# Two transformer blocks in one kernel: where the weight tiles lie behind the moving tiles, and output projections by three matmuls

## The chip, the cores and the metric

The kernel runs on one core of a Trainium2 chip. The metric is the device time of one execution in microseconds (us), the median of the runs shown. TensorE (PE) does the matmuls, and its weight loads are listed apart (PEld). VectorE (DVE) and ScalarE (ACT) do the elementwise work, GpSimd (POOL) little, and SyncE (SP) issues the weight transfers.

## The reference

Two blocks follow each other on x of 256 tokens by 1024, each of two layers, all in float32.

```python
# first block, per layer
proj = rms_norm(x, norm_mix[l]) @ w_in[l]                # 1024 -> 5120
x = x + (gates * (attention_a @ w_proj_a, attention_b @ w_proj_b)) @ w_out[l]
up = rms_norm(x, norm_ffn[l]) @ w_up[l]                  # 1024 -> 2 x 2816
x = x + (silu(conv(a)) * bval) @ w_down[l]               # 2816 -> 1024
# second block, per layer
y = even_mixer(h) or odd_mixer(h)                        # ends in @ w_out, 1024 -> 1024
x = x + rms_norm_2(y, g[1]);  y = memory_cross_attention(h, mem)
x = x + rms_norm_2(y, g[3]);  y = jnp.square(jax.nn.relu(h @ w1)) @ w2    # 1024 -> 4096 -> 1024
x = x + rms_norm_2(y, g[5])
```

Nearly all of the arithmetic is products of a weight matrix with activations of 256 tokens.

## The kernel before, in words

Activations stand transposed: features on the 128 partitions, 256 tokens along a row. To keep float32 accuracy every operand is split into a rounded part (hi) and a rest (lo), both of type float32r, and a product is hi·hi + lo·hi + hi·lo. `mm3` (L239 to L243) issues these three matmuls of 256 columns for one tile of 128 by 128 weights: weights hi on tokens hi, weights lo on tokens hi, weights hi on tokens lo. In most projections the weights are the stationary operand, which TensorE loads (one LDWEIGHTS for each matmul), and the tokens (`xh`, or `ya`, `yb`, `ox`) are the moving one. `proj_n` is the other way round: weights move, 512 columns at a time.

`plan` lists the 434 weight blocks in the order of use. `prep` (L188 to L201) loads one into a `raw` tile (three buffers, SP's queue), and for each half of it lets ACT write the hi part (L199) and DVE the lo part (L200) of a tile `w`, of which there are WB = 8. `take` hands a block to a projection and prepares blocks up to LEAD = 5 ahead; `hold(True)` stops this at the end of the matrix in work.

The output projections (`w_out`, `w_down`, `ev_out`, `od_out`, `w2`) end in `proj_tail` (L367 to L376): eight chunks of 128 output features, or the last four of `ev_out` and `od_out` (`OutFirst` does their first 512 features by `mm3`, in banks `mo`). Seven of them go through `proj_wide` and `mm3_wide` (L245 to L248), which do one tile of weights by two matmuls: weights hi on 512 columns (tokens hi and lo side by side), then weights lo on 256 columns. The bank `mw` then holds two partial sums, which DVE and ACT add up: `on_part` in `residual` (L871 to L883, additions in L875 and L877) or `Output.part` (L1336 to L1351, a copy by ACT in L1343 and an addition in L1344). The last chunk goes through `proj_c`, by `mm3` in half a bank. A matrix of `w_down` has 22 tiles per chunk, `w2` 32, the others 8.

The order on each engine is made by a scheduler that simulates the program's time line, which may take matmuls of a later chunk ahead of those of an earlier one.

Where tiles lie, as built: a pool gives all buffers of a tag slots of one size, that of the largest tile under the tag. The largest `w` tile is that of a block of 260 columns, 2·2·260·4 = 4160 bytes, which is 16·256 + 64, and the slots begin at byte 39552 of a partition. So the eight slots begin at 128, 192, 0, 64, 128, 192, 0, 64 modulo 256. The tiles of moving tokens are 4096 bytes each: the tag `xs` (input of `w_in`, `w_up`, `w1`) begins at 83072, 128 modulo 256, and `hs` (input of the output projections) at 154944, 64 modulo 256. Rows, halves and columns inside a tile are multiples of 256 bytes apart. So for each weight tile there is one distance "weights behind tokens, modulo 256": 0, 64, 128 or 192, each for about a quarter of the matmuls. For the stretches that the rows below show:

| stretch from (us) | weights at | tokens at | behind | the tile just before |
|---|---|---|---|---|
| 949.46 | 43712 | 95360 | 64 | 128 behind |
| 950.88 | 68672 | 91264 | 192 | 64 behind |
| 952.28 | 60352 | 87168 | 64 | 192 behind |
| 953.64 | 52032 | 83072 | 192 | 64 behind |
| 272.55 (two tiles) | 60352, 43712 | 87168, 83072 | 64 | 192 behind |
| 275.28 | 56192 | 95360 | 0 | 64 behind |
| 276.71 | 47872 | 91264 | 128 | 0 behind |
| 278.14 | 52032 | 87168 | 192 | 128 behind |
| 630.43 | 52032 | 87168 | 192 | 0 behind |
| 1255.94 (two tiles) | 60352, 43712 | 87168, 83072 | 64 | 0 behind |
| 1263.06 (two tiles) | 52032, 68672 | 83072, 95360 | 192 | 128 behind |

Each of these tiles serves 12 matmuls of 256 columns.

Of the kernel before, what the change touches and what calls it, by code (L numbers as in the profile page):

```python
# [32 lines left out]
TWO_PI = (6.28125, 0.0019350051879882812, 3.0199159819567e-07)  # L33
LEAD = 5
WB = 8
TCARGS = dict(schedule_with_timeline_sim=True)
SET_EXP = "natural_log_exp_and_others"

# [77 lines left out]
def starts(blocks):  # L116

    out = [0]
    for _, _, nk, _, C in blocks:
# [1 line left out]
    return out  # L121


BUFS = {"x": 5, "xs": 4, "hs": 16, "ft": 7, "sq": 2, "p": 6, "bias": 3, "row": 4, "sm": 16, "mk": 2, "mv": 2,
        "mm": 2, "sc": 2, "pT": 2, "pv": 1, "ms": 1}


# [1 line left out]
def net(ctx, tc, A, out):  # L129
    nc = tc.nc  # L130
    act, dve, pe, pool = nc.scalar, nc.vector, nc.tensor, nc.gpsimd
    cp = ctx.enter_context(tc.tile_pool(name="const", bufs=1))
    wp = ctx.enter_context(tc.tile_pool(name="wts", bufs=1))
    ap = ctx.enter_context(tc.tile_pool(name="acts", bufs=1))
    pp = ctx.enter_context(tc.tile_pool(name="psum", bufs=1, space=PSUM))
    dp = ctx.enter_context(tc.tile_pool(name="dram", bufs=1, space=DRAM))

    def f(x):
        return x.bitcast(F32)

# [43 lines left out]
    start = starts(W)  # L184
    state = {"n": 0, "next": 0, "limit": len(W), "after": None, "sum": None}
    ready = {}

    def prep(i, pieces=1):  # L188
        name, k0, nk, c0, C = W[i]
        raw = wp.tile([P, nk, C], F32, tag="raw", name=f"raw{i}", bufs=3)  # L190
        src = A["wt"][start[i]:start[i] + P * nk * C].rearrange("(p k c) -> p k c", p=P, k=nk)
        for a in range(0, nk, max(1, nk // pieces)):
            nc.sync.dma_start(raw[:, a:a + max(1, nk // pieces)], src[:, a:a + max(1, nk // pieces)])
        h = max(1, nk // 2)
        ready[i] = []
        for a, b in ((0, h), (h, nk)):
            if a < b:
                w = wp.tile([P, 2, b - a, C], F32R, tag="w", name=f"w{i}", bufs=WB)
                act.activation(w[:, 0], raw[:, a:b], AF.Copy)  # L199
                dve.tensor_tensor(w[:, 1], raw[:, a:b], f(w[:, 0]), op=OP.subtract)  # L200
                ready[i] += [w[:, :, k] for k in range(b - a)]  # L201

    def take(name, c0, k0=0):

        i = state["n"]
        assert (W[i][0], W[i][3], W[i][1]) == (name, c0, k0), (W[i], name, c0, k0)
        state["n"] += 1
        ahead()
        return ready.pop(i)
# [25 lines left out]
    def mm(o, a, b, start, stop):  # L235
        i = pe.matmul(o, a, b, start=start, stop=stop, skip_group_check=True).ins  # L236
        if state["after"] is not None:
            no_sync(i, state["after"])

    def mm3(o, l, r, start, stop=True):  # L240

        for n, (a, b) in enumerate(((0, 0), (1, 0), (0, 1))):
            mm(o, l[:, a], r[:, b], start and n == 0, stop and n == 2)  # L243

    def mm3_wide(o, l, r, start, stop):  # L245

        mm(o, l[:, 0], r, start, False)
        mm(o[:, 0:T], l[:, 1], r[:, 0], False, stop)  # L248

    def cut(w, s):  # L250
        return w[:, :, s]
# [63 lines left out]
    def proj_c(name, c0, x, k=KC, tag="mm"):  # L315

        ps = bank(tag, "mm", (T,))
        for k0 in range(0, k, 8):
            w = take(name, c0, k0)
            for kk in range(min(8, k - k0)):  # L320
                mm3(ps, w[kk], x(k0 + kk), start=(k0 + kk == 0), stop=(k0 + kk == k - 1))
        return ps

    def proj_wide(name, c0, x, k, tag):

        ps = bank(tag, "mw")
        for k0 in range(0, k, 8):
            w = take(name, c0, k0)
            for kk in range(min(8, k - k0)):
                mm3_wide(ps.rearrange("p a t -> p (a t)"), w[kk], x(k0 + kk), start=(k0 + kk == 0),  # L330
                         stop=(k0 + kk == k - 1))
        return ps

    def proj_n(name, c0, x, C=256, tag="mm"):

        if C <= 256:
# [27 lines left out]
        def later(self, k0):  # L364
            return lambda: self(k0)

    def proj_tail(name, x, k, on_part, tags=("mm", "sc", "mm", "sc", "mm", "sc", "mm", "sc"), first=0):  # L367

        for c in range(first, 8):
            if c == 4:  # L370
                hold(True)
            if c < 7:
                ps = proj_wide(name, 128 * c, x, k, tags[c])
                on_part(c, ps[:, 0], ps[:, 1])
            else:
                on_part(c, proj_c(name, 128 * c, x, k, tags[c]), None)  # L376


    xt = A["xT"].rearrange("(k p) t -> p k t", p=P)
    x = [sb("x", f"x{j}") for j in range(4)]  # L380
# [15 lines left out]
    def const(name, shape, q=nc.sync):  # L396
        t = cp.tile(list(shape), F32, name=name)
        q.dma_start(t, A[name])
        return t
# [14 lines left out]
    class Sums:  # L414
# [8 lines left out]
        def part(self, s, last=False):  # L423
            first = self.ps is None
            if first:
                self.ps = bank("ms", "ssum", (T,))
            state["sum"] = pe.matmul(self.ps, ones, s, start=first, stop=last).ins  # L427
# [184 lines left out]
        return t[hh * 64:hh * 64 + 64, c]  # L612


    h = Split("xs")
    for c in range(8):
        split_last = h.chunk(c, x[c // 2][:, c % 2], vcol(V_MIX + c))

    def first_sums():
# [4 lines left out]
        ns.chunk(x[3][:, 1])  # L624
        return ns

    exchange = const("exchange", [P, P], nc.gpsimd)
    table = const("table", [32, 28], nc.gpsimd)
    sink = cp.tile([P, 16], F32, name="sink")
# [38 lines left out]
    for l in range(DEPTH):  # L668
        vb = l * V_L1
        w_in = f"w_in{l}"  # L670
        def rope_unit(nat):
            ra = sb("sm", "ra", (2, 4, 2, 8))
            rb = sb("sm", "rb", (2, 4, 2, 8))
            for i in range(2):
                rt = nat[:, i].rearrange("p (h d) -> p h d", h=4)[:, :, 0:16]
                rt = rt.rearrange("p h (b r) -> p h b r", b=2)
                dve.tensor_tensor(ra[:, i], rt, trig[:, 0, i][:, None].to_broadcast([P, 4, 2, 8]), op=OP.mult)
                for b in range(2):
                    dve.tensor_tensor(rb[:, i, :, b], rt[:, :, 1 - b],
                                      trig[:, 1, i, b][:, None].to_broadcast([P, 4, 8]), op=OP.mult)  # L680
                dve.tensor_tensor(rt, ra[:, i], rb[:, i], op=OP.add)
            pt = bank("pT", "qT")
            for c in range(2):
                for i in range(2):
                    tr(pt[:, c, col(i)], nat[:, i, col(c)])
            s = single("rope", "qTs")
            act.activation(s, pt, AF.Copy)
            return s
# [17 lines left out]
        o = unit(0)  # L706
# [143 lines left out]
        for j in range(4):  # L850
# [3 lines left out]
            for w, y, g, tag in ((pa, ya, gates[j], "mm"), (pb, yb, gates[4 + j], "pT")):  # L854
                o = bank(tag, "mm")
# [9 lines left out]
        def residual(w, y, k, gains):  # L865

            hn = Split("xs") if gains is not None else None
            ns = Sums()
            xn = []

            def on_part(c, a, b):  # L871
                if c % 2 == 0:
                    xn.append(sb("x", f"x{c // 2}"))
                t = xn[c // 2][:, c % 2]
                state["block1"] = dve.tensor_tensor(t, x[c // 2][:, c % 2], a, op=OP.add).ins  # L875
                if b is not None:
                    dve.tensor_tensor(t, t, b, op=OP.add)  # L877
                if c < 6 and c % 2:
                    ns.pair(xn[c // 2])
                if hn is not None:  # L880
                    hn.chunk(c, t, gains(c))
                if c >= 6:
                    ns.chunk(t)  # L883

            proj_tail(w, y, k, on_part)
            hold(False)
            return xn, hn, ns
# [4 lines left out]
        for j in range(11):  # L892
# [6 lines left out]
            a = sb("ft", "fa")  # L899
# [58 lines left out]
    hm = mem_operand(0, mem)  # L958


    lprod = sb("sm", "lp", (64,))
    lsum = sb("sm", "ls", (2,))
    for j in range(2):
        no_sync(dve.tensor_tensor_reduce(lprod, lamv[:, 2 * j], lamv[:, 2 * j + 1], 1.0, 0.0, op0=OP.mult,
# [60 lines left out]
    xn = []  # L1025
# [284 lines left out]
    class Output:  # L1310
# [22 lines left out]
            self.sums.chunk(ps)  # L1333
            self.scale(self.ys[3][:, c % 2], ps, c)

        def part(self, c, a, b):  # L1336
            if b is None:
                self.chunk(c, a)
                return
            if c % 2 == 0:  # L1340
                self.ys.append(sb("ft", "y"))
            y = self.ys[c // 2]
            act.activation(y[:, c % 2], b, AF.Copy)  # L1343
            dve.tensor_tensor(y[:, c % 2], a, y[:, c % 2], op=OP.add)  # L1344
            if c == 6:
                self.sums.chunk(y[:, 0])
                self.scale(y[:, 0], y[:, 0], c)
            elif c % 2:
                self.sums.pair(y)
                for i in range(2):  # L1350
                    self.scale(y[:, i], y[:, i], c - 1 + i)  # L1351

    def close(y, r):

# [14 lines left out]
    for l in range(DEPTH):  # L1369
        name, oo, of = even(h, nrm) if l == 0 else odd(h, nrm)  # L1370
        y = Output(lambda c: gain2(l, 1, c), 2)
        for j in range(2):
            y.pair(j, of.banks[j])
        proj_tail(name, oo, KC, y.part, tags=(None,) * 4 + ("sc", "mm", "sc", "mm"), first=4)
        r = y.sums.rows(1)
        mem_keys(l, hm, mk, 1)
        xn = []
# [156 lines left out]
```

## Time and profile before

| what | us |
|---|---|
| median of 3 runs | 1434.24 (1433.52 to 1435.65) |
| the profiled execution: its time | 1434.43 |
| the profiled execution: its span, from first to last instruction | 1432.3 |
| TensorE busy | 1388.8 |
| DVE busy | 1019.8 |
| ACT busy | 886.3 |

Busy time is the union of an engine's instructions. Matmuls are pipelined: one of 256 columns takes some 283 ns from start to end, and the next starts long before it ends. So what a matmul costs in a stream is read from the starts: of n matmuls in an unbroken row, the row's time less one duration, over n - 1.

### The profile page before, as it was taken

The numbers are of one execution on the slowest core, as the hardware profiler recorded it, in microseconds if no ns is written. First come the engines' busy times: TensorE is split into PE (matmuls) and PEld (weight loads), VectorE is DVE, ScalarE is ACT, GpSimd is POOL, SyncE is SP. The second block draws the span as 40 slices with busy tenths as digits, with TensorE's granted clock in tenths as the row PEclk, the third lists the DMA queues.
The fourth block names the chain that finished last, engine by engine and source line by source line (L and its number), as shares of the span: only waits on it lengthen the run. The fifth ranks groups of instructions, "written<-read, shape, count | busy, mean of one in ns | idle before, by whom it ended". The sixth has DMA issues, their size and how long they took to land.

```text
span 1432.3 us, 26226 instructions
## 1 busy us (share of the span) xinstructions
PE 1388.8 (97%) x9950; PEld 1270.7 (89%) x9950; DVE 1019.8 (71%) x2140; ACT 886.3 (62%) x1740; POOL 27.3 (2%) x54
## 2 busy tenths in 40 slices
PE   8999999999999999999999989899999999899997
PEld 6789999998888999999899968799989878799886
DVE  6665888886656578888777786777656876777554
ACT  6666566665566666666656656566556676576553
POOL 1000000000000000000000010000000010000000
PEclk9999999999999999999999989999999999999999
DMA  7543566556653455656655553266656534265662
GB/s 247 187 124 119 182 195 191 188 177 188 192 170 119 127 172 188 193 190 198 198 167 164 154 139 118 75 190 186 186 187 180 161 94 133 82 186 189 182 189 85
DMA packets 69326, 236.14 MB, mean 165 GB/s; under 512 B 7954, under 2 KB 12322, under 8 KB 69200
## 3 DMA queue, kind: packets, MB, share of 16 engines
q1 hardware_dynamic: 67136, 229.24, 51.6%
q0 software_dynamic: 1920, 5.04, 1.8%
q8 instruction: 78, 1.28, 0.4%
q14 instruction: 48, 0.39, 0.1%
q10 hardware_dynamic: 144, 0.19, 0.0%
HBM read 233.35 MB, written 1.09 MB: 164 GB/s over the span
## 4 chain that ended last, share of the span: by engine, by line
issue 53%; PE 39%; DVE 3%; ACT 3%; DMA 1%; POOL 0%; SPq 0%; DVEq 0%; POOLq 0%; ACTq 0%
PE mm L236 21%; PE mw L236 12%; PE mo L236 2%; PE ssum L427 1%; PE pT L483 1%; PE sc L607 1%; PE sc L604 1%; ACT w L199 1%; DVE w L200 1%; PE pv L541 1%; DMA bias<-brel_d 1%; DMA x<-in_xT_dram 0%; ACT rstd L176 0%; ACT sq L431 0%; ACT px L176 0%
## 5 line engine op out<-in xcount | busy, mean ns | idle before, releaser
L200 DVE TENSOR_TENSOR w<-raw,w 128x512 fp32r<-128x512 f32 (+2 forms) x866 | 585.3, 686 | 303.3 <-ACT w L199 292.8
L199 ACT ACTIVATE w<-raw 128x512 fp32r<-128x512 f32 (+2 forms) x866 | 535.5, 626 | 414.6 <-PE mm L236 225.5
L236 PE MATMUL mm<-xh,w 128*128 128x256 f32 x5892 | 722.8, 283 | 7.8 <-ACT xh L1000 6.8
L236 PEld LDWEIGHTS mm<-xh,w 128*128 128x128 f32 x5892 | 703.7, 190 | 21.2 <-ACT xh L1000 8.4
L236 PE MATMUL mw<-xh,w 128*128 128x512 f32 (+1 forms) x1832 | 327.3, 339 | 2.4 <-DVE xh L271 1.4
L236 PEld LDWEIGHTS mw<-xh,w 128*128 128x128 f32 x1832 | 281.2, 188 | 44.6 <-DVE xh L271 2.0
L236 PE MATMUL mm<-w,xh 128*128 128x512 f32 (+2 forms) x672 | 145.8, 372 | 9.5 <-ACT w L199 7.0
L236 PEld LDWEIGHTS mm<-w,xh 128*128 128x128 f32 x672 | 113.6, 191 | 34.0 <-ACT w L199 8.4
L236 PE MATMUL mo<-xh,w 128*128 128x256 f32 x192 | 30.6, 307 | 0.5 <-ACT xh L513 0.5
L236 PEld LDWEIGHTS mo<-xh,w 128*128 128x128 f32 x192 | 26.5, 206 | 4.4 <-ACT xh L513 1.7
L1000 ACT ACTIVATE xh<-x,vec 128x256 fp32r<-128x256 f32 x48 | 22.6, 501 | 10.4 <-DVE x L1365 9.9
L497 POOL DMA_DIRECT2D bias<-brel_d x28 | 14.9, 538 | 680.0 <-DVE sbb L821 293.0
L905 ACT ACTIVATE ftt<-fa,vec 128x256 f32<-128x256 f32 x44 | 24.1, 594 | 2.3 <-DVE fa L900 0.5
L1003 DVE SCALAR_TENSOR_TENSOR xh<-x,vec,xh 128x256 fp32r<-128x256 f32 x48 | 22.1, 483 | 1.1 <-ACT xh L1000 1.1
L431 ACT ACTIVATE sq<-x 128x512 f32<-128x512 f32 x33 | 20.4, 617 | 2.3 <-DMA x<-in_xT_dram 2.1
L906 DVE SCALAR_TENSOR_TENSOR ftt<-fa,vec,ftt 128x255 f32<-128x255 f32 x44 | 20.9, 482 | 0.2
L907 DVE SCALAR_TENSOR_TENSOR ftt<-fa,vec,ftt 128x254 f32<-128x254 f32 x44 | 21.0, 477 | 0.0
L703 DVE TENSOR_TENSOR gate<-mm,rstd 128x512 f32<-128x512 f32 x16 | 11.1, 691 | 12.5 <-PE mm L236 12.5
L438 DVE TENSOR_TENSOR sq<-sq 128x512 f32<-128x512 f32 x26 | 17.9, 688 | 0.0
L176 ACT ACTIVATE ftt<-ftt 128x512 f32<-128x512 f32 x22 | 13.9, 631 | 6.4 <-DVE ftt L907 6.4
L1364 DVE TENSOR_TENSOR y<-y,rstd 128x512 f32<-128x512 f32 (+1 forms) x25 | 14.5, 581 | 4.3 <-ACT rstd L176 4.1
L910 DVE TENSOR_TENSOR fa<-mm,rstd 128x512 f32<-128x512 f32 x22 | 15.1, 687 | 3.1 <-PE mm L236 3.1
(413 smaller groups left out, 1137.2 us busy)
## 6 DMA issues: line engine op xcount, KB each, us to landing
raw<-in_wt_dram SPq DMA_DIRECT2D x411, 512.0 KB, 3.6
raw<-in_wt_dram SPq DMA_DIRECT2D x16, 384.0 KB, 3.5
bias<-brel_d POOLq DMA_DIRECT2D x28, 128.0 KB, 3.4
raw<-in_wt_dram SPq DMA_DIRECT2D x4, 520.0 KB, 3.5
mem<-in_memT_dram SPq DMA_DIRECT2D x8, 256.0 KB, 4.2
x<-in_xT_dram SPq DMA_DIRECT2D x4, 256.0 KB, 6.7
raw<-in_wt_dram SPq DMA_DIRECT2D x4, 256.0 KB, 3.3
out_dram<-y SPq DMA_DIRECT2D x4, 256.0 KB, 2.5
```

The lines of the kernel that those rows point to most:

```text
L199: act.activation(w[:, 0], raw[:, a:b], AF.Copy)
L200: dve.tensor_tensor(w[:, 1], raw[:, a:b], f(w[:, 0]), op=OP.subtract)
L236: i = pe.matmul(o, a, b, start=start, stop=stop, skip_group_check=True).ins
L431: act.activation(sq, src, AF.Square)
L438: dve.tensor_tensor(self.acc, self.acc, sq, op=OP.add)
L497: nc.gpsimd.dma_start(o, src)
L905: act.activation(t[:, c], a[:, c], AF.Identity, bias=vcol(vb + V_CB + ch), scale=w[2])
L906: dve.scalar_tensor_tensor(t[:, c, 1:], a[:, c, :T - 1], w[1], t[:, c, 1:], op0=OP.mult, op1=OP.add)
L907: dve.scalar_tensor_tensor(t[:, c, 2:], a[:, c, :T - 2], w[0], t[:, c, 2:], op0=OP.mult, op1=OP.add)
L910: dve.tensor_tensor(a, o, over(rr), op=OP.mult)
L1000: act.activation(hi, t, AF.Copy, scale=g)
L1003: return dve.scalar_tensor_tensor(lo, t, g, f(hi), op0=OP.mult, op1=OP.subtract)
```

## The change

Weight slots become 4224 bytes (`W_SLOT` = 1056 elements, 16·256 + 128), so that they begin at 128 and 0 modulo 256 in turn. Two unused tiles (`pad`) of 192 and 64 bytes, and a tag `ro` of its own for three small tiles that made the slots of `sm` large, move the other pools: `xs` then begins at 83776 and `hs` at 150592, both 64 modulo 256. Every weight tile is then 64 or 192 bytes behind the moving tile. `proj_wide` and `mm3_wide` go; `proj_tail` uses `mm3` for every chunk. Chunks 0 to 5 share a bank in pairs, where only the first matmul of the first chunk starts a sum, and 6 and 7 have a bank each. `on_part` gets a pair or a single chunk, and no partial sums are left to add.

```diff
+W_SLOT = 1056
...
-BUFS = {"x": 5, "xs": 4, "hs": 16, "ft": 7, "sq": 2, "p": 6, "bias": 3, "row": 4, "sm": 16, "mk": 2, "mv": 2,
+BUFS = {"x": 5, "xs": 4, "hs": 16, "ft": 7, "sq": 2, "p": 6, "bias": 3, "row": 4, "sm": 16, "ro": 4, "mk": 2, "mv": 2,
...
+    def pad(name, n):
+        ap.tile([P, n // 4], F32, tag=name, name=name, bufs=1)
...
-                w = wp.tile([P, 2, b - a, C], F32R, tag="w", name=f"w{i}", bufs=WB)
+                w = wp.tile([P, W_SLOT], F32R, tag="w", name=f"w{i}", bufs=WB)
+                w = w[:, :2 * (b - a) * C].rearrange("p (s k c) -> p s k c", s=2, k=b - a)
...
-    def mm3_wide(o, l, r, start, stop):
-        mm(o, l[:, 0], r, start, False)
-        mm(o[:, 0:T], l[:, 1], r[:, 0], False, stop)
...
-    def proj_tail(name, x, k, on_part, tags=("mm", "sc", "mm", "sc", "mm", "sc", "mm", "sc"), first=0):
+    def proj_tail(name, x, k, on_part, tags=("mm", "sc", "mm", "sc", "mm"), first=0):
+        tags = list(tags)
+        cs, ps = [], None
         for c in range(first, 8):
             if c == 4:
                 hold(True)
-            if c < 7:
-                ps = proj_wide(name, 128 * c, x, k, tags[c])
-                on_part(c, ps[:, 0], ps[:, 1])
-            else:
-                on_part(c, proj_c(name, 128 * c, x, k, tags[c]), None)
+            if not cs:
+                ps = bank(tags.pop(0), "mw", (2, T) if c < 6 else (1, T))
+            for k0 in range(0, k, 8):
+                w = take(name, 128 * c, k0)
+                for kk in range(min(8, k - k0)):
+                    mm3(ps[:, len(cs)], w[kk], x(k0 + kk), start=(k0 + kk == 0 and not cs),
+                        stop=(k0 + kk == k - 1))
+            cs.append(c)
+            if c % 2 or c >= 6:
+                on_part(cs, ps)
+                cs = []
...
+    pad("pad0", 192)
     h = Split("xs")
...
+    pad("pad1", 64)
     exchange = const("exchange", [P, P], nc.gpsimd)
...
-            ra = sb("sm", "ra", (2, 4, 2, 8))
-            rb = sb("sm", "rb", (2, 4, 2, 8))
+            ra = sb("ro", "ra", (2, 4, 2, 8))
+            rb = sb("ro", "rb", (2, 4, 2, 8))
...
-            def on_part(c, a, b):
+            def on_part(cs, ps):
+                c = cs[0]
                 if c % 2 == 0:
                     xn.append(sb("x", f"x{c // 2}"))
-                t = xn[c // 2][:, c % 2]
-                state["block1"] = dve.tensor_tensor(t, x[c // 2][:, c % 2], a, op=OP.add).ins
-                if b is not None:
-                    dve.tensor_tensor(t, t, b, op=OP.add)
+                s = slice(c % 2, c % 2 + len(cs))
+                state["block1"] = dve.tensor_tensor(xn[c // 2][:, s], x[c // 2][:, s], ps, op=OP.add).ins
...
-        def part(self, c, a, b):
-            if b is None:
-                self.chunk(c, a)
-                return
...
+        def part(self, cs, ps):
+            if len(cs) == 2:
+                self.pair(cs[0] // 2, ps)
+            else:
+                self.chunk(cs[0], ps[:, 0])
```

TensorE at the start of the first `w_out`, before. Here w_1684, w_1734, w_1742 and w_1814 are the first halves of the weights of chunks 0 to 3, and xh the mixed attention output, which is still being made.

```order
L236 MATMUL mm<-yb,w_1655 128x256 x3
L236 MATMUL mw<-xh,w_1734 128x512
L236 MATMUL mw<-xh,w_1734 128x256
L236 MATMUL mw<-xh,w_1734 128x512
L236 MATMUL mw<-xh,w_1684 128x512
L236 MATMUL mw<-xh,w_1684 128x256
L236 MATMUL mw<-xh,w_1684 128x512
L236 MATMUL mw<-xh,w_1684 128x256
L236 MATMUL mw<-xh,w_1734 128x256
L236 MATMUL mw<-xh,w_1742 128x512
L236 MATMUL mw<-xh,w_1814 128x512
```

The same place in the changed kernel. Here w_1686 and w_1689 are the two halves of chunk 0, w_1744 and w_1747 those of chunk 2, w_1824 the first half of chunk 4, and w_1736 that of chunk 1.

```order
L242 MATMUL mw<-xh,w_1686 128x256 x6
L242 MATMUL mw<-xh,w_1744 128x256
L242 MATMUL mw<-xh,w_1686 128x256 x2
L242 MATMUL mw<-xh,w_1744 128x256 x7
L242 MATMUL mw<-xh,w_1686 128x256 x4
L242 MATMUL mw<-xh,w_1689 128x256 x2
L242 MATMUL mw<-xh,w_1744 128x256 x4
L242 MATMUL mw<-xh,w_1747 128x256 x2
L242 MATMUL mw<-xh,w_1824 128x256
L242 MATMUL mw<-xh,w_1689 128x256 x4
```

Before, the first four chunks are open at once. Now chunks 0, 2 and 4 are, each in a bank of its own, and chunk 1 follows when chunk 0 is complete; w_1824 lies in the slot that w_1686 leaves.

DVE in the first `w_down`, before, from the end of chunk 0 to that of chunk 1. The w_ rows are lo parts of weights, x the new residual, xh the lo part of the next operand.

```order
L875 TENSOR_TENSOR x_3834<-x_1917,mw 128x256
L877 TENSOR_TENSOR x_3834<-x_3834,mw 128x256
L200 TENSOR_TENSOR w_3795<-raw_3790,w_3795 128x512
L200 TENSOR_TENSOR w_3816<-raw_3814,w_3816 128x512
L279 SCALAR_TENSOR_TENSOR xh<-x_3834,vec,xh 128x256
L200 TENSOR_TENSOR w_3819<-raw_3814,w_3819 128x512
L200 TENSOR_TENSOR w_3843<-raw_3841,w_3843 128x384
L200 TENSOR_TENSOR w_3846<-raw_3841,w_3846 128x384
L200 TENSOR_TENSOR w_3867<-raw_3865,w_3867 128x512
L875 TENSOR_TENSOR x_3834<-x_1917,mw 128x256
L200 TENSOR_TENSOR w_3870<-raw_3865,w_3870 128x512
L877 TENSOR_TENSOR x_3834<-x_3834,mw 128x256
```

And in the changed kernel, at the end of the pair of chunks 0 and 1:

```order
L206 TENSOR_TENSOR w_3935<-raw_3933,w_3935 128x512
L878 TENSOR_TENSOR x_3991<-x_1959,mw 128x512
L206 TENSOR_TENSOR w_3938<-raw_3933,w_3938 128x512
L280 SCALAR_TENSOR_TENSOR xh<-x_3991,vec,xh 128x256 x2
L206 TENSOR_TENSOR w_3967<-raw_3965,w_3967 128x512
```

Four additions of 128x256 have become one of 128x512, after both chunks.

## Rows read from the trace of the kernel before

**Rows 1.** The page, parts 1 and 2: busy time by engine; TensorE's granted clock
```profile
PE 1388.8 (97%) x9950; PEld 1270.7 (89%) x9950; DVE 1019.8 (71%) x2140; ACT 886.3 (62%) x1740; POOL 27.3 (2%) x54
...
PEclk9999999999999999999999989999999999999999
```

**Rows 2.** Groups: line engine op names shapes count | busy us, mean ns | idle before
```profile
L236 PE MATMUL mm<-xh,w 128*128 128x256 f32 x5892 | 722.8, 283 | 7.8 <-ACT xh L1000 6.8 <-ACT w L199 0.5 <-DVE xh L1003 0.4
...
L236 PE MATMUL mw<-xh,w 128*128 128x512 f32 (+1 forms) x1832 | 327.3, 339 | 2.4 <-DVE xh L271 1.4 <-ACT y L1321 0.5 <-DVE mx L1196 0.5
...
L236 PE MATMUL mo<-xh,w 128*128 128x256 f32 x192 | 30.6, 307 | 0.5 <-ACT xh L513 0.5
...
L236 PE MATMUL mm<-ya,w 128*128 128x256 f32 x96 | 12.6, 281 | 0.0
...
L199 ACT ACTIVATE w<-raw 128x512 fp32r<-128x512 f32 (+2 forms) x866 | 535.5, 626 | 414.6 <-PE mm L236 225.5 <-PE mw L236 122.0 <-DMA raw<-in_wt_dram 30.5
```

**Rows 3.** Timeline, TensorE, merged matmuls: start us, us, line op names count
```profile
200.51 112.86 PE L236 MATMUL mm<-xh,w 128*128 128x256 f32 x960
...
599.73 76.78 PE L236 MATMUL mm<-xh,w 128*128 128x256 f32 x659
...
938.95 61.29 PE L236 MATMUL mm<-xh,w 128*128 128x256 f32 x520
...
1253.85 77.45 PE L236 MATMUL mm<-xh,w 128*128 128x256 f32 x651
...
313.21 54.25 PE L236 MATMUL mw<-xh,w 128*128 128x512 f32 x308
...
1015.52 79.07 PE L236 MATMUL mw<-xh,w 128*128 128x512 f32 x448
...
167.01 17.64 PE L236 MATMUL mw<-xh,w 128*128 128x512 f32 x99 [0.72 <-DVE xh L271]
```

**Rows 4.** Timeline, TensorE, four weight tiles in succession, first w1 stage
```profile
949.46 1.46 PE L236 MATMUL mm<-xh,w 128*128 128x256 f32 x11
...
950.88 1.46 PE L236 MATMUL mm<-xh,w 128*128 128x256 f32 x11
...
952.28 1.41 PE L236 MATMUL mm<-xh,w 128*128 128x256 f32 x11
...
953.64 1.41 PE L236 MATMUL mm<-xh,w 128*128 128x256 f32 x11
```

**Rows 5.** Timeline, TensorE, tiles of the first w_up stage
```profile
272.55 2.77 PE L236 MATMUL mm<-xh,w 128*128 128x256 f32 x23
...
275.28 1.48 PE L236 MATMUL mm<-xh,w 128*128 128x256 f32 x11
...
276.71 1.47 PE L236 MATMUL mm<-xh,w 128*128 128x256 f32 x11
...
278.14 1.46 PE L236 MATMUL mm<-xh,w 128*128 128x256 f32 x11
```

**Rows 6.** Timeline, TensorE, tiles of the second w_up and w1 stages
```profile
630.43 1.41 PE L236 MATMUL mm<-xh,w 128*128 128x256 f32 x11
...
1255.94 2.88 PE L236 MATMUL mm<-xh,w 128*128 128x256 f32 x23
...
1263.06 2.87 PE L236 MATMUL mm<-xh,w 128*128 128x256 f32 x23
```

**Rows 7.** Windows, first w_up: us, busy PE PEld DVE ACT POOL, PEclk, DMA
```profile
201.00:313.00 112.00, 112.00 (x958) 112.00 (x957) 96.48 (x165) 72.18 (x123) 1.62 (x3) 1.00 0.59 186
```

**Rows 8.** Groups: the additions that end the projections of two matmuls
```profile
L875 DVE TENSOR_TENSOR x<-x,mw 128x256 f32<-128x256 f32 x28 | 11.7, 417 | 4.5 <-PE mw L236 4.5
...
L877 DVE TENSOR_TENSOR x<-x,mw 128x256 f32<-128x256 f32 x28 | 11.7, 417 | 0.1
...
L1344 DVE TENSOR_TENSOR y<-mw,y 128x256 f32<-128x256 f32 x20 | 8.4, 418 | 0.0
```

**Rows 9.** Waits of TensorE: who, for whom, us in total, times, longest
```profile
PE mm L236 <- ACT w L199: 7.5, 4, 6.1
```

More of the change, by code (lines that the diff above doesn't have):

```diff
@@ L322, in proj_c @@
         return ps
[L324 to L332, printed above, removed]
     def proj_n(name, c0, x, C=256, tag="mm"):
@@ L869, in residual @@
             xn = []
-            def on_part(c, a, b):
+            def on_part(cs, ps):
+                c = cs[0]
                 if c % 2 == 0:
                     xn.append(sb("x", f"x{c // 2}"))
-                t = xn[c // 2][:, c % 2]
-                state["block1"] = dve.tensor_tensor(t, x[c // 2][:, c % 2], a, op=OP.add).ins
-                if b is not None:
-                    dve.tensor_tensor(t, t, b, op=OP.add)
-                if c < 6 and c % 2:
-                    ns.pair(xn[c // 2])
[L880 to L883, printed above, removed]
+                s = slice(c % 2, c % 2 + len(cs))
+                state["block1"] = dve.tensor_tensor(xn[c // 2][:, s], x[c // 2][:, s], ps, op=OP.add).ins
+                if c < 6:
+                    ns.pair(xn[c // 2])
+                for c in cs:
+                    t = xn[c // 2][:, c % 2]
+                    if hn is not None:
+                        hn.chunk(c, t, gains(c))
+                    if c >= 6:
+                        ns.chunk(t)
             proj_tail(w, y, k, on_part)
@@ L958, in net @@
     hm = mem_operand(0, mem)
-    lprod = sb("sm", "lp", (64,))
+    lprod = sb("ro", "lp", (64,))
     lsum = sb("sm", "ls", (2,))
@@ L1334, in chunk @@
             self.scale(self.ys[3][:, c % 2], ps, c)
-        def part(self, c, a, b):
-            if b is None:
-                self.chunk(c, a)
-                return
[L1340 to L1351, printed above, removed]
+        def part(self, cs, ps):
[3 more added lines that the diff above has]
+                self.chunk(cs[0], ps[:, 0])
     def close(y, r):
@@ L1373, in net @@
             y.pair(j, of.banks[j])
-        proj_tail(name, oo, KC, y.part, tags=(None,) * 4 + ("sc", "mm", "sc", "mm"), first=4)
+        proj_tail(name, oo, KC, y.part, tags=("sc", "mm", "sc"), first=4)
         r = y.sums.rows(1)
```

## The prediction

> **What bounds the kernel now.** First the busy times. TensorE is busy for 1388.8 of 1432.3 us, and its granted clock was at nine tenths or more of full speed in all slices but one [rows 1]. DVE and ACT have about 30% and 40% of the span left. Then who waits for whom. ACT sits idle 414.6 us ahead of the weight copies of L199, and most of that, 225.5 and 122.0 us, ends with a matmul that gives a weight buffer back [rows 2]. TensorE, the other way round, waited 7.5 us in all for such a copy [rows 9]. So weights are ready early, and the kernel is as long as TensorE's stream of matmuls, with pauses between stages. The question is what one matmul costs in that stream.
>
> Busy time doesn't tell that, so I read the time line. In an unbroken row of n matmuls the interval from start to start is (time - 0.283)/(n - 1), with 283 ns for the last one [rows 2]. Four long rows give 117.4, 116.3, 117.5 and 118.7 ns [rows 3]; by their counts 117.5 ns. They differ, although the instructions in them are alike in form. The short rows show why: a stretch over one or two weight tiles has an interval of its own, and neighbouring tiles differ. Held against the table of distances:
>
> - 0 behind: (1.48 - 0.283)/10 = 120 ns; 128 behind: 119 ns [rows 5].
> - 64 and 192 behind: either (2.77 - 0.283)/22 = 113 ns [rows 5] or 118 ns [rows 4, 5, 6].
>
> The two values at 64 and 192 are two paces of the stream, and what sets the pace is what came before. After a tile at 128, a tile at 192 goes at 118 ns [rows 5, 6]; after 0, one at 64 goes at 118 ns and one at 192 at 113 ns [rows 6]. Rows 4 matter most, since there four tiles follow each other as they will after the change, 64, 192, 64, 192: (1.46 - 0.283)/10 = 118, 118, then (1.41 - 0.283)/10 = 113, 113 ns [rows 4]. The step from 192 to 64 brings the quick pace, and the step from 64 to 192 keeps whatever pace there is. The two tiles of rows 5 at 113 ns come after a tile at 192 too.
>
> **The changed parts, one by one.**
>
> *A. Distances, for the matmuls that stay.* Those of 256 columns under `mm` and `mo`, with three groups of 96 (ya shown, yb and ox alike), are 5892 + 192 + 288 = 6372 [rows 2]. Now a quarter stands at each distance and the mean is 117.5 ns. Afterwards there is no 0 and no 128. I take 113.2 ns for the quick pace and 117.7 for the other one. A pause can set the slower pace, and it stays until the next step from 192 to 64, which comes within some two to four tiles, or 24 to 48 matmuls. The long rows of 520 to 960 matmuls without a pause [rows 3] should be quick nearly throughout; short pieces in the attention stages, perhaps half. I choose three quarters at the quick pace: 0.75 x 113.2 + 0.25 x 117.7 = 114.3 ns. That is 6372 x 3.2 ns = 20.4 us off TensorE's stream, all on the path.
>
> *B. Three matmuls for two.* `mw` has 1832 matmuls, so 916 pairs of 512 and 256 columns [rows 2]. A row of 308 took 54.25 us: less 0.283 for the last and some 0.234 for a single 512, 53.73/153 = 351 ns a pair; the row of 448 gives 78.55/223 = 352 ns [rows 3]. I take 351.5. Three matmuls at 114.3 are 343 ns, a gain of 8.5 ns x 916 = 7.8 us. At 117.7 they would be 353 ns and lose 1.5 us in all; with every one quick, 339.6 ns, a gain of 10.9 us. The third weight load lies beside the matmuls, as in every `mm` row.
>
> *C. No partial sums to add.* The additions of L877 and L1344, 11.7 and 8.4 us of DVE [rows 8], go, with ACT's copies for them, and the additions of L875 are made in pairs. They lie beside TensorE's work, so I cost them at nothing: chunks 0 to 5 are read while later chunks run, and the last chunk ends as it did.
>
> *D. Order at `w_out`.* TensorE has to fill the time until the last pair of the mixed operand is made. Before, four chunks were open, and one pause was 0.72 us [rows 3]. Now three are, and chunk 4's weights go into the slot that chunk 0 leaves, so an ACT copy of 0.626 us [rows 2] and DVE's pass lie between. The cost is bounded by 0 and by the six tiles of chunk 1 that can't fill in, 6 x 0.35 = 2.1 us. I take 1 us in each of the two layers, 2 us.
>
> *E. Smaller tiles in `ro`, pads, wider slots.* They issue nothing. The rotary units reuse four slots in DVE's own order, so I cost this at nothing.
>
> *F. Faster TensorE, same weight work.* In the first `w_up` DVE is busy 96.48 of 112 us [rows 7]. At 113.2 ns the stage would take some 108 us, with DVE at 89%. Cover is left, but less of it.
>
> Sum: -20.4 - 7.8 + 2 = -26.2 us on the profiled execution of 1434.43 us, which stands 0.2 us above the median: **1408 us**.
>
> **What speaks against it.** The chief objection is that addresses should not matter at all. The row shows that they do: 120 ns at distance 0, 113 at 64, one after the other in one stage [rows 5]. The Trainium skill ("SBUF — State Buffer", section "Who interferes with whom") gives TensorE two independent read ports, for the moving operand and for weights, and has it wait for nobody. By that, A would be worth nothing; the trace disagrees, 120 against 113 ns. The Trainium skill ("TensorE: Matmul & The Clock Gate", section "Back-to-back issue gap") has N/2.4 + 2.5 ns for an isolated gap, which gives 325 ns for the pair and 327.5 for three, so that B would lose an estimated 2.3 us. The trace has 351.5 for the pair and 339 to 353 for three.
>
> **Rivals.**
>
> *1. The distance is not the cause,* and the intervals follow something else that the change leaves alone. Three matmuls at the mean of 117.5 are 352.5 ns: +0.9 us, and D's 2 us: 1437 us at most, 1435 without D. For it: the same distance has two values. Against it: a tile at 0 never went at 113 ns in the rows read. Chance 0.06.
>
> *2. Quick only in the 256-wide stages.* The tails have tiles of 128 columns, four rows of weights to a half, and token tiles that change every matmul triple; no row at hand shows them at 113 ns. Then A stays and B loses 1.5 us: 1434.4 - 20.4 + 1.5 + 2 = 1417.5 us. Chance 0.17. If instead DVE starved TensorE in `w_up`, what A gives there would go: 22 projections of 48 matmuls in each of two layers, 2112 x 3.2 ns = 6.8 us, so 1415 us. Chance 0.04.
>
> *3. Slower: the pace of 118 ns holds.* A pause or the odd order of buffers sets it, and alternation keeps it, as it did over the first two tiles of rows 4 and over two tiles each in rows 6. A then gives 6372 x -0.2 ns, +1.3 us; B +1.5 us; D +2 us: 1439 us. It decides where fewer than one matmul in ten or so comes to the quick pace. Against it: rows 4 and 5 leave that pace at 192 to 64, and the change is full of such steps. Chance 0.06.
>
> *Forecast,* the quick pace in both kinds of stage, share a half to nearly all: chance 0.67. With every matmul quick it would be 1434.4 - 27.4 - 10.9 = 1396 us; with half of them, 115.5 ns, A 12.7 and B 4.6 us, 1419 us.
>
> **The numbers.** A measurement tells some 0.2% from no change, 2.9 us, so faster means under 1431.4. The forecast and rival 2 are faster, 0.88; rival 1 is mostly within, 0.06; rival 3 slower, 0.06. The range runs from 1396, all quick, to 1420, which takes in rival 2; what is left out is rivals 1 and 3 and a little at the ends, under 0.2.
>
> **What would show it.** In the profile after, the long `mm` rows should stand at 113 to 115 ns, the first `w_up` (960 matmuls) in 108.5 to 110 us where it took 112.86. The tails' rows should show 340 to 345 ns for three, the first `w_down`'s 154 products of chunks 0 to 6 in some 53 us. No stretch should show 119 or 120 ns. The row of L1344 should be gone and DVE's busy time lower by some 20 us. The forecast is wrong if the long rows stay at 117 to 118 ns, or if TensorE's waits for weights grow well over 7.5 us.

## The result, and the profile after

The changed kernel takes 1408.28 us in the median of 4 runs (1406.38 to 1410.85); the kernel before took 1433.88 us in the runs beside it (1433.16 to 1435.65). The ratio is 0.9821, with an interval of 0.9801 to 0.984. The forecast was 1408.0. The profiled execution took 1410.85 us, the longest of the four, with a span of 1409.1 us; against the profiled execution of before, 1434.43, that is 23.6 us less, where the sum of the prediction had 26.2.

The page, parts 1 and 2, of the kernel after (they answer to [rows 1]):

```profile
PE 1360.9 (97%) x10866; PEld 1283.0 (91%) x10866; DVE 1001.3 (71%) x2080; ACT 880.1 (62%) x1720; POOL 27.7 (2%) x54
...
PEclk9999999999999999999999989999999999899999
```

TensorE runs 916 matmuls more and is busy 27.9 us less. Its share of the span is 97% as before, so it still sets the length. DVE's busy time is 18.5 us lower, where some 20 were expected.

The groups of the kernel after (they answer to [rows 2] and [rows 8]):

```profile
L205 ACT ACTIVATE w<-raw 128x512 fp32r<-128x512 f32 (+2 forms) x866 | 534.5, 627 | 387.4 <-PE mm L242 188.0
L242 PE MATMUL mm<-xh,w 128*128 128x256 f32 x5472 | 653.8, 280 | 8.0 <-ACT xh L1003 6.9
...
L242 PE MATMUL mw<-xh,w 128*128 128x256 f32 x3168 | 367.1, 277 | 5.4 <-DVE xh L272 3.7
...
L878 DVE TENSOR_TENSOR x<-x,mw 128x512 f32<-128x512 f32 (+1 forms) x20 | 11.5, 573 | 0.1
```

All the matmuls under `mw` have 256 columns now: 3 times 916, and 420 of chunk 7 that stood under `mm`. L878 makes 20 additions, pairs among them, where L875 and L877 made 56; the second additions, L1344 too, are gone. ACT still idles 387 us ahead of its weight copies, mostly for buffers: weights are still early.

The timeline of the kernel after, TensorE's long rows in the order of the run (they answer to [rows 3]; start us, us, line, operation, count):

```profile
205.12 103.74 PE L242 MATMUL mm<-xh,w 128*128 128x256 f32 x912
308.70 60.00 PE L242 MATMUL mw<-xh,w 128*128 128x256 f32 x528
...
599.78 66.12 PE L242 MATMUL mm<-xh,w 128*128 128x256 f32 x582
665.74 60.01 PE L242 MATMUL mw<-xh,w 128*128 128x256 f32 x528
...
926.45 73.82 PE L242 MATMUL mm<-xh,w 128*128 128x256 f32 x648
1000.44 87.21 PE L242 MATMUL mw<-xh,w 128*128 128x256 f32 x768
...
1237.00 74.16 PE L242 MATMUL mm<-xh,w 128*128 128x256 f32 x651
1310.99 87.21 PE L242 MATMUL mw<-xh,w 128*128 128x256 f32 x768
```

With the interval as the prediction read it, the first row gives (103.74 - 0.28)/911 = 113.6 ns where its like before had 117.4, and 960 matmuls would take 109.2 us where they took 112.86. The other `mm` rows give 113.3, 113.7 and 113.7 ns. All four `mw` rows, the two `w_down` stages and the two `w2` stages, give 113.3 ns: 340 ns for three, where the pair took 351 to 352.

The windows of the kernel after, most of the first `w_up` (as [rows 7]: us, busy PE, PEld, DVE, ACT, POOL, granted clock, DMA share, GB/s):

```profile
197.00:306.00 109.00, 109.00 (x955) 108.03 (x955) 95.42 (x164) 71.84 (x122) 1.63 (x3) 1.00 0.66 196
```

DVE is busy 88% of it and TensorE all of it.

TensorE's waits in the kernel after (for whom, us in total, times, longest; the first answers to [rows 9]):

```profile
PE mm L242 <- ACT w L205: 8.6, 3, 6.5
...
PE mw L242 <- DVE xh L272: 3.7, 4, 1.3
...
PE mw L242 <- DVE mx L1199: 1.7, 1, 1.7
```

Waits for weights stand at 8.6 us, beside 7.5 before. What grew is the wait for the mixed operand at `w_out` (`xh`, 1.4 us before [rows 2]), and the one wait for `mx` in the third row, which was 0.5.

To close the sum I added up, for every matmul with a weight tile as its stationary operand, the time from its start to the next start, and counted what is more than 15 ns above the usual interval as a pause. The last line of the table takes the pauses at all matmuls of TensorE, those of attention too.

| | before | after |
|---|---|---|
| 256 columns outside the pairs: count, mean ns | 6384, 117.4 | 5964, 114.2 |
| 512 and 256 columns of a pair, ns | 233.2 + 118.4 | none |
| `mw`, all 256 columns: count, mean ns | none | 3168, 113.55 |
| pauses at all matmuls, us | 119.5 | 126.4 |

The matmuls outside the pairs give back 5964 x 3.2 ns + 420 x 3.8 ns = 20.6 us, and the pairs 916 x (351.6 - 340.65) ns = 10.0 us. The pauses take 6.9 us. That is 23.7 us less, and 23.6 were measured. Where the line between an interval and a pause is drawn moves the pauses' term by some 2 us, so that the sum closes to 0.1 us is partly luck.

### The profile page after: what moved, and what is told of

Read it like the earlier page. It is cut to its first block, busy times and chain, and to the rows that moved or that the text cites. A ratio compares the mean times of both kernels' runs of the same rounds, so it can differ in the third digit from the quotient of the medians.

```text
span 1409.1 us, 27993 instructions
## 1 busy us (share of the span) xinstructions
PE 1360.9 (97%) x10866; PEld 1283.0 (91%) x10866; DVE 1001.3 (71%) x2080; ACT 880.1 (62%) x1720; POOL 27.7 (2%) x54
## 4 chain that ended last, share of the span: by engine, by line
issue 53%; PE 36%; DVE 5%; ACT 4%; DMA 1%; POOL 0%; SPq 0%; DVEq 0%; POOLq 0%; ACTq 0%
PE mm L242 18%; PE mw L242 13%; PE mo L242 1%; ACT w L205 1%; PE ssum L427 1%; DVE w L206 1%; DMA bias<-brel_d 1%; PE pT L483 1%; PE pv L541 1%; ACT y L1324 0%; DMA raw<-in_wt_dram 0%; ACT sq L431 0%; ACT rstd L181 0%; ACT px L181 0%; DVE work L1140 0%
## 5 line engine op out<-in xcount | busy, mean ns | idle before, releaser
L242 PE MATMUL mm<-xh,w 128*128 128x256 f32 x5472 | 653.8, 280 | 8.0 <-ACT xh L1003 6.9
L242 PEld LDWEIGHTS mm<-xh,w 128*128 128x128 f32 x5472 | 636.0, 189 | 20.8 <-ACT xh L1003 8.5
L242 PE MATMUL mw<-xh,w 128*128 128x256 f32 x3168 | 367.1, 277 | 5.4 <-DVE xh L272 3.7
L242 PEld LDWEIGHTS mw<-xh,w 128*128 128x128 f32 x3168 | 362.8, 188 | 7.5 <-DVE xh L272 4.5
L438 DVE TENSOR_TENSOR sq<-sq 128x512 f32<-128x512 f32 x26 | 17.8, 685 | 0.4
L524 ACT ACTIVATE pT0s<-pT 128x512 f32<-128x512 f32 x18 | 10.7, 596 | 10.4 <-PE pT L483 10.4
```

The source lines that it names most:

```text
L438: dve.tensor_tensor(self.acc, self.acc, sq, op=OP.add)
```

## The experiments

In each, the ratio is to the kernel before on the same chip. Where a number is called an interval, it is (row - 0.283)/(count - 1) as above.

**Distances alone** (`e1_phase_only`): the kernel before with the new slots, pads and `ro`, and the pairs of 512 and 256 columns kept.

```diff
+W_SLOT = 1056
...
-                w = wp.tile([P, 2, b - a, C], F32R, tag="w", name=f"w{i}", bufs=WB)
+                w = wp.tile([P, W_SLOT], F32R, tag="w", name=f"w{i}", bufs=WB)
+                w = w[:, :2 * (b - a) * C].rearrange("p (s k c) -> p s k c", s=2, k=b - a)
...
+    pad("pad0", 192)
...
+    pad("pad1", 64)
```

> The placement alone: weight slots of 4224 bytes, pads and small tiles as in the change, but the output projections still by one matmul of 512 and one of 256 columns. Theory (the distance sets the pace): the 6372 matmuls of 256 columns that stay go from 117.5 to about 114 ns, -20 to -24 us; the 916 pairs gain 0 to 5 ns each, 0 to -5 us; the order at w_out is that of before, so no new pause: 1406 to 1414 us. Rival (the distance is not the cause, three matmuls for two are): 1434 us, the long mm rows still at 117 to 118 ns.

Measured: 1417.88 us (1416.45 to 1418.82) against 1434.65, ratio 0.9889 (0.9872 to 0.9905). The timeline of this kernel:

```profile
199.82 108.17 PE L242 MATMUL mm<-xh,w 128*128 128x256 f32 x951
307.83 54.50 PE L242 MATMUL mw<-xh,w 128*128 128x512 f32 x308
...
1002.17 79.25 PE L242 MATMUL mw<-xh,w 128*128 128x512 f32 x448
```

The distances alone bring 16.8 us, in the 256-wide stages: 113.6 ns. The pairs gain nothing, and by the sums lose about 1 ns each. With the prediction's own reckoning, (54.50 - 0.517)/153 = 353 ns a pair, beside 351 before [rows 3]. By the sums over all starts a 256 that follows a 512 takes 119.0 ns here, at distances of 64 and 192 alone. So the 512-column matmul keeps the stream off the quick pace, and the part of the change that I had priced as "three for two" is what lets the tails have it.

**Three matmuls alone** (`e2_three_only`): the kernel after with the slots of before and without pads and `ro`.

```diff
-                w = wp.tile([P, W_SLOT], F32R, tag="w", name=f"w{i}", bufs=WB)
-                w = w[:, :2 * (b - a) * C].rearrange("p (s k c) -> p s k c", s=2, k=b - a)
+                w = wp.tile([P, 2, b - a, C], F32R, tag="w", name=f"w{i}", bufs=WB)
...
-    pad("pad0", 192)
...
-    pad("pad1", 64)
```

> The three matmuls alone: output projections as in the change, weight slots and pools as before, so a quarter of the tiles at each distance. Theory: three at the mean of 117.5 ns are 352.5 against 351.5 ns for the pair, +1 us, and the order at w_out costs 2 to 3 us: 1435 to 1439 us. Rival (the gain is that of three matmuls or of the additions left out): 1426 us or less.

Measured: 1436.46 us (1434.89 to 1438.15), ratio 1.0013 (1.0004 to 1.0022). Its timeline:

```profile
206.84 106.91 PE L241 MATMUL mm<-xh,w 128*128 128x256 f32 x912
313.59 62.05 PE L241 MATMUL mw<-xh,w 128*128 128x256 f32 x528
...
1018.47 90.50 PE L241 MATMUL mw<-xh,w 128*128 128x256 f32 x768
```

The intervals are 117.0, 117.2 and 117.6 ns, three for 351 to 353 ns. This is the arithmetic of rival 1: at the old distances three matmuls cost what the pair costs, or a little more. TensorE's waits for the mixed operand at `w_out` are 3.3 us here, beside 1.4 before, so the stage order has its part in the 1.8 us. The two parts by themselves give -16.8 and +1.8 us, a sum of -15.0; both in one kernel give -25.6. Some 10 us belong to neither alone.

**The other two distances** (`e3_dist_0_128`): the kernel after, 64 bytes more in a pad that nothing reads, so that weights lie 0 and 128 behind in turn.

```diff
-    pad("pad0", 192)
+    pad("pad0", 256)
```

> The changed kernel with the tokens' tiles moved by 64 bytes more, so that the weights are 0 and 128 bytes behind in turn; nothing else differs. Theory: all 9132 matmuls with stationary weights go at 118.5 to 120 ns instead of 114, +41 to +54 us on the changed kernel: 1450 to 1463 us. Rival (wider slots, two distances in turn or the smaller pools are the cause): 1408 us as the changed kernel.

Measured: 1451.61 us (1450.29 to 1453.23), ratio 1.0122 (1.0107 to 1.0137). Its timeline:

```profile
210.34 108.95 PE L242 MATMUL mm<-xh,w 128*128 128x256 f32 x912
319.13 63.07 PE L242 MATMUL mw<-xh,w 128*128 128x256 f32 x528
```

Intervals of 119.3 and 119.1 ns. The same instructions in the same order take 43 us longer for 64 bytes of address. Rival 1, that the distance is not the cause, falls here. The Trainium skill ("SBUF — State Buffer", section "Who interferes with whom") has two independent read ports for TensorE and lets it wait for nobody; this run disagrees, by about 6 ns a matmul.

The pad moves the tokens and leaves the weights, so this run by itself could also mean that the tokens' own place matters. The trace of e2 tells the two apart, since its tiles stand at all four distances, with tokens at 64 and at 128 modulo 256. By the sums over all starts, tiles 0 behind have a mean of 119.7 ns with tokens at either place, tiles 128 behind 118.5 and 118.6, and tiles 64 or 192 behind 115.0 to 115.9. The interval goes with the distance and not with either address.

**One distance only** (`e4_all_64`, `e5_all_192`): slots of 4352 bytes, so that all weight tiles begin alike modulo 256. Then there is no step from 192 to 64, or back, between tiles. The first edit is e4, both are e5.

```diff
-W_SLOT = 1056
+W_SLOT = 1088
...
-    pad("pad0", 192)
+    pad("pad0", 320)
```

> The changed kernel with slots of 4352 bytes and tokens placed so that every weight tile is 64 bytes behind. Theory (distance and history): after a pause a tile at 64 goes at 113 ns more often than not (in the trace of before 9 of 12 times), and no step changes the pace until the next pause; so a mixture, more quick than not: 1404 to 1420 us, with whole stretches between pauses at one pace. Rival (only 64 and 192 in turn give the quick pace): 118 ns nearly throughout, 1438 us or more.

Measured: 1417.67 us (1414.55 to 1419.65), ratio 0.9873 (0.9847 to 0.9899).

> The changed kernel with slots of 4352 bytes and tokens placed so that every weight tile is 192 bytes behind. Theory (the pace depends on the distance and on what came before): after a pause a tile at 192 goes at 118 ns, and with no step from 192 to 64 nothing ends that, so nearly all of the 9132 matmuls go at 117.7 instead of 114 ns, +34 us: 1438 to 1444 us. Rival (64 and 192 are good distances by themselves): 1408 us.

Measured: 1426.6 us in 9 runs (1421.16 to 1435.23), ratio 0.9948 (0.9925 to 0.9972). A miss: I had the 118 ns pace nearly throughout. The timeline of e5:

```profile
206.60 107.68 PE L242 MATMUL mm<-xh,w 128*128 128x256 f32 x912
314.12 62.35 PE L242 MATMUL mw<-xh,w 128*128 128x256 f32 x528
...
1258.83 74.13 PE L242 MATMUL mm<-xh,w 128*128 128x256 f32 x651
1332.80 87.21 PE L242 MATMUL mw<-xh,w 128*128 128x256 f32 x768
```

And that of e4:

```profile
205.17 107.68 PE L242 MATMUL mm<-xh,w 128*128 128x256 f32 x912
312.69 62.35 PE L242 MATMUL mw<-xh,w 128*128 128x256 f32 x528
...
672.30 60.01 PE L242 MATMUL mw<-xh,w 128*128 128x256 f32 x528
```

Whole stages stand at 117.9 ns, others at 113.3 to 113.6, in both kernels, at one distance each. Taken tile by tile in order: in e5, of 603 successions of tiles without a pause between them, 462 kept 118 and 141 kept 113, and none changed. In e4 the counts are 173 and 410, and again none changed. What a stretch gets is drawn at the pause before it: 113 ns after 8 of 75 pauses in e5, after 44 of 76 in e4. That would also explain why e5's runs lie 14 us apart; only one of the nine was traced, so it isn't shown. In the kernel after, 17 of 19 tiles at 64 that followed a tile of 192 at 118 ns went over to 113 to 115 ns; all 5 tiles of 192 that followed one of 64 at 117 or 118 stayed at 118; and none of 340 steps in either direction left 113. So the rule that I had read from four tiles [rows 4] holds, with exceptions: the step from 192 to 64 mostly brings the quick pace, and the step from 64 to 192 keeps what there is. It isn't the only step that does so. In e2, among tiles that follow each other without a pause, a tile at 118 to 120 ns was followed by one at 113 in 56 of 56 steps from 0 to 192, in 52 of 60 from 128 to 64 and in 21 of 27 from 192 to 64, but in none of 28 from 0 to 64, of 41 from 128 to 192 and of 13 from 64 to 192. Alternation is worth 9 us over the better single distance.

**Distances between** (`e7_dist_32_160`, `e8_dist_96_224`): the kernel after with `pad0` of 224 and of 160 bytes.

```diff
-    pad("pad0", 192)
+    pad("pad0", 224)
```

> The changed kernel with the tokens' tiles moved by 32 bytes, so that the weights are 32 and 160 bytes behind in turn, distances that no row of before or after shows. Theory (a collision of the two reads that depends on the distance) gives no sure number: between 113 and 120 ns, 1405 to 1460 us; if the grain is 64 bytes the pace is that of 0 and 128 or of 64 and 192, if it is finer something between. Rival (the distance is not the cause): 1408 us.

> As the run with 32 and 160 bytes, but 96 and 224 bytes behind in turn. Theory: between 113 and 120 ns, 1405 to 1460 us; together with 32 and 160 it tells the grain of the distance. Rival (the distance is not the cause): 1408 us.

Measured: e7 1451.93 us (1450.46 to 1454.32), ratio 1.0119 (1.009 to 1.0148); e8 1437.61 us in 10 runs (1434.44 to 1442.54), ratio 1.0016 (1.0 to 1.0032). Their first `w_up`, e7 ahead of e8, each from its own timeline:

```profile
208.79 108.92 PE L242 MATMUL mm<-xh,w 128*128 128x256 f32 x912
```

```profile
208.20 107.07 PE L242 MATMUL mm<-xh,w 128*128 128x256 f32 x912
```

119.3 and 117.2 ns. Over all intervals without a wait, 32 behind has a mean of 118.2 ns, 96 118.0, 160 119.9 and 224 116.7, beside 119.6 at 0 and 118.6 at 128 (e3). So 32 bytes already change the interval, and of eight distances only 64 and 192 hold long rows at 113 ns.

**A bank for each chunk at `w_out`** (`e6_wout_banks`): the kernel after, where in the two `w_out` stages alone four chunks are open again, as before the change, each with a bank of its own.

```diff
-                ps = bank(tags.pop(0), "mw", (2, T) if c < 6 else (1, T))
+                ps = bank(("mm", "sc")[c % 2] if alone else tags.pop(0), "mw", (2, T) if c < 6 and not alone else (1, T))
...
-            if c % 2 or c >= 6:
+            if c % 2 or c >= 6 or alone:
...
-            proj_tail(w, y, k, on_part)
+            proj_tail(w, y, k, on_part, alone=w.startswith("w_out"))
```

> The changed kernel with a bank for each chunk in w_out alone, so that its first four chunks are open at once as before; placement and three matmuls as in the change. Theory (the order at w_out costs the pauses of 1.50 and 0.78 us in the first layer and 1.47 and 0.78 us in the second that the changed kernel shows there, where before it was one of 0.88 and 0.85): 2 to 3 us less than the changed kernel, 1405 us. Rival (the mixed operand comes when it comes, and the pause only moves): 1408 us.

Measured: 1406.09 us (1405.77 to 1406.47), ratio 0.9794 (0.9773 to 0.9816). That is 2 us from the change, but its chip had not run the change itself, so the next two runs have both on one chip.

> The changed kernel itself once more, beside the next two on the same chip: 1406 to 1411 us.

> The changed kernel with a bank for each chunk in w_out, once more. Theory (the order at w_out costs pauses): 2 to 3 us under the changed kernel of this call. Rival (it was the spread of the runs): the same.

Measured: the change again (`e9_change_again`) 1407.13 us (1404.68 to 1408.84), ratio 0.9805 (0.9793 to 0.9818); the banks again (`e10_wout_again`) 1403.95 (1401.75 to 1405.65), ratio 0.9782 (0.9769 to 0.9795). The first `w_out` up to the first `w_up` in e9:

```profile
163.63 2.18 PE L242 MATMUL mw<-xh,w 128*128 128x256 f32 x16
...
167.12 1.90 PE L242 MATMUL mw<-xh,w 128*128 128x256 f32 x13 [1.31 <-DVE xh L272]
...
169.53 18.78 PE L242 MATMUL mw<-xh,w 128*128 128x256 f32 x163 [0.51 <-DVE xh L272]
188.15 5.61 PE L242 MATMUL mm<-xh,w 128*128 128x256 f32 x48
```

And in e10:

```profile
161.84 3.00 PE L242 MATMUL mw<-xh,w 128*128 128x256 f32 x25
165.33 19.27 PE L242 MATMUL mw<-xh,w 128*128 128x256 f32 x167 [0.49 <-DVE xh L272]
184.43 5.15 PE L242 MATMUL mm<-xh,w 128*128 128x256 f32 x44
```

In e9 TensorE has 16 matmuls to do, waits 1.31 us for the mixed operand, has 13 more, and waits again for the last pair; from first product to `w_up` it takes 24.52 us. In e10 the fourth chunk gives it 25 in the first piece, one wait of 0.49 us is left, and the stage takes 22.59 us. In the second layer, from first product to `w_up`, it takes 24.48 and 22.54 us. So the pairing of banks costs 1.9 us at each of the two `w_out` stages. In the first layer 1.33 us of that is idle time (1.31 + 0.51 us beside 0.49); the rest lies in the matmuls beside the pauses, several of which start some 180 to 230 ns apart. The version with banks, which is e6's kernel again, is the quickest of all here; by medians it is 3.2 us ahead of the change, and the run ranges overlap a little.

**Distance 64 for every first half, 192 for every second** (`e11_halves`): e10 with the two halves of a unit in slots of their own, four each, so that every unit has its step from 64 to 192 and every next one the step back.

```diff
-W_SLOT = 1056
+W_SLOT = 1088
...
-                w = wp.tile([P, W_SLOT], F32R, tag="w", name=f"w{i}", bufs=WB)
+                t = "w" if a == 0 else "v"
+                if a and "v" not in slots:
+                    wp.tile([P, 32], F32, tag="wpad", name="wpad", bufs=1)
+                slots.add(t)
+                w = wp.tile([P, W_SLOT], F32R, tag=t, name=f"w{i}", bufs=WB // 2)
...
-    pad("pad0", 192)
+    pad("pad0", 64)
```

> As the run before, and the two halves of each weight block in slots of their own tag, four each, of 4352 bytes, the first half always 64 and the second always 192 bytes behind. Theory (history): a pause mostly falls ahead of a first half, which goes at 113 ns more often than not, and otherwise the next step from 192 to 64 comes two tiles on; the share of matmuls at 117 to 119 ns falls from about 9 to 5 in 100, worth 1 to 2 us: 1404 us. Rival (which tile follows a pause doesn't matter): the same as the run before. That two buffers of a kind have to be free instead of any two could add waits for weights, up to a few us.

Measured: 1410.9 us in 6 runs (1406.09 to 1419.65), ratio 0.9837 (0.9815 to 0.986): 7 us behind e10, a miss. The intervals hardly moved (114.15 ns outside `mw` and 113.47 under it, in e10 114.24 and 113.49), so the steps had almost nothing left to win. In the profiled executions the pauses grew by 17.8 us; e11's is the longest of its six and e10's the shortest of its four. Most of that is one stretch. Windows of e11, in the last attention stage (columns as above):

```profile
1125.00:1130.00 5.00, 3.35 (x24) 2.71 (x23) 5.00 (x22) 3.87 (x14) 1.26 (x3) 1.00 0.45 138
1130.00:1135.00 5.00, 5.00 (x25) 3.06 (x24) 4.97 (x26) 3.98 (x17) 1.56 (x3) 0.70 0.68 159
1135.00:1140.00 5.00, 5.00 (x21) 3.99 (x20) 1.29 (x8) 0.29 (x1) 1.07 (x2) 0.50 0.33 75
1140.00:1145.00 5.00, 5.00 (x19) 2.79 (x18) 3.83 (x17) 3.23 (x12) 0.00 (x0) 0.50 0.01 2
```

Its timeline there:

```profile
1129.68 0.49 PE L609 MATMUL sc<-kv,qo 64*128 64x128 f32 x2 [1.64 <-DVE mx L1257]
...
1137.57 2.05 PE L247 MATMUL mo<-xh,w 128*128 128x256 f32 x8
```

And e10's at the same place in the program:

```profile
1122.86 0.48 PE L604 MATMUL sc<-kv,qo 64*128 64x128 f32 x2 [0.72 <-DVE mx L1252]
...
1128.22 1.17 PE L242 MATMUL mo<-xh,w 128*128 128x256 f32 x8
```

In the first of these windows TensorE was busy for 3.35 of 5 us; its wait for DVE, 1.64 us where e10 had 0.72, ends there. In the windows after that the granted clock is 0.70 and then 0.50, the level of 1.2 GHz, and the same eight matmuls take 2.05 us for 1.17; in e10 it stays at 1.00 from 1115 to 1135 us. From the wait for weights ahead of this stage to the wait ahead of the next `w1` e11 takes 135.6 us and e10 123.5. Ahead of this, DVE had waited for a bias transfer. The first row is e11's, the second e10's at the same place:

```profile
1122.79 0.69 DVE L509 TENSOR_TENSOR bias<-bias,m_band 128x512 f32<-128x512 f32 x1 [2.34 <-DMA bias<-brel_d]
```

```profile
1114.57 0.69 DVE L504 TENSOR_TENSOR bias<-bias,m_band 128x512 f32<-128x512 f32 x1 [0.19 <-DMA bias<-brel_d]
```

From that row on DVE in e11 worked without a gap until TensorE's wait was over. Why the bias came late, whether the edit had a part in it, and what the other runs of e11 lost, stays open. ACT's waits for weight transfers stand at 73.3 us in e11 and 32.4 in e10, so the weights came later with the halves in fixed slots; TensorE's own wait for weights hardly changed, 7.0 and 8.1 us.

## Why the prediction was right, point by point

- **What bounds the kernel:** right. Busy share 97% before and after, and the time followed the interval of the matmuls in e1 to e5, e7 and e8; e6, e10 and e11 differ from the change by their pauses.
- **The rule of steps** (192 to 64 brings the quick pace, 64 to 192 keeps the pace): right for most steps, 17 of 19 in the kernel after and 21 of 27 in e2. It had rested on four tiles and two more, so that it held is in part luck. That a pause can set the slower pace was an assumption, for which the prediction shows no row; e5 bears it out, with 118 ns after 67 of 75 pauses.
- **A, distances, -20.4 us:** right, 20.6 by the sums. The mean is 114.2 ns where 114.3 was taken; the long rows are quick from end to end, and the short pieces between pauses hold the rest. With the pairs kept (e1) the same matmuls give some 20 us by the sums, and the whole kernel 16.8.
- **B, three for two, -7.8 us:** right in sign, too small: 10.0. I gave the tails the mean of the attention pieces, 114.3, though they are rows of 528 and 768 matmuls without a pause; they stand at 113.55. The term that was mis-sized is that of the three, 343 ns, which measure 340.65; the pair's 351.5 was right, and e1 shows that the pair gets no better at the new distances (353). So A and B are not two independent terms: B is worth 10 us only with A, and nothing without it, where e2, with D in it, lost 1.8 us.
- **C, additions, 0:** right; DVE's 18.5 us changed no row of TensorE, and e2, which has no such additions either, gained nothing.
- **D, order at `w_out`, +2 us:** right in kind, half the size: 3.9 us by e9 and e10. I bounded it by the six tiles of chunk 1 that can't fill in, 2.1 us a layer, and took the middle; nearly the whole bound is paid, 1.9 us a layer. There are two waits, 1.3 and 0.5 us, where before there was one of 0.7, and each wait also spreads the matmuls beside it.
- **E, smaller tiles and pads, 0:** not told apart; every run with the new distances has them too.
- **F, weight work as cover:** right. TensorE waits 8.6 us for weights, beside 7.5, with DVE at 88% of the first `w_up`.
- **What the sum lacked:** about 3 us of pauses outside `w_out`. The granted clock may account for some of it: its mean is 0.988 in this execution and 0.990 before, a shortfall from full speed of 16.7 and 13.7 us over the span. The repeat (e9) has 0.991, 13.3 us, and its profiled execution took 1407.13.
- **Rival 1** fell by e3. **Rival 2** fell by the `mw` rows at 113.3 ns, and its second form by the waits for weights. **Rival 3,** the 118 ns pace that holds, is real, but it holds whole stages only where steps from 192 to 64 are missing, in e4 and e5. In the kernel after it holds a tile or a few behind a pause.

The errors of B and D have opposite signs and nearly cancel; the forecast of 1408.0 lies 0.3 us from the median while B and D are each some 2 us off, and that is luck. The lower end of the prediction's range, 1396, leaves out D's 2 us, which the other times have.

Open: why the interval depends on the distance at all, why some steps bring the quick pace and others don't, and why a pause draws one pace or the other. Distances finer than 32 bytes weren't tried.

## What to carry to other kernels

Where TensorE is the bound, read the interval from unbroken rows of equal matmuls, not the busy time, and compare it between tiles: if equal instructions differ by several per cent, look at where their operands lie, and shift a pool by a few dozen bytes. Test a pair of edits apart and together, since one may pay only in the presence of the other. When a bank or buffer is saved at the head of a stage, count the work that filled the wait there.

## What was not expected of the hardware

- At one distance there are two stable paces, 113.3 and 117.9 ns; without a pause 1186 successions of tiles kept theirs, in e4 and e5. The Trainium skill ("TensorE: Matmul & The Clock Gate", section "Back-to-back issue gap") has N/2.4 + 2.5 ns for an isolated gap, an estimated 109.2 ns at 256 columns; no long row of any run was below 113.3.
- A 512-column matmul takes a stream off the quick pace: the 256 behind it takes 119.0 ns, at distances where 256 behind 256 goes at 113 to 114 (e1).
- The grain of the distance is 32 bytes or less: 0, 32, 64 give 119.6, 118.2 and 113 ns or 118.
- One longer wait of TensorE, 1.64 us for 0.72, was followed by some 20 us at a granted clock of 0.50, and the stage took 12 us longer than in e10 (e11).
